# Diagonal queries and keys of stick-breaking attention in separate tiles, queries loaded through SyncE; the scan written in place

## The chip, the cores and the metric

The kernel runs on one core of a Trainium2 chip. The core's engines are TensorE (PE; its weight loads are listed as PEld), VectorE (DVE), ScalarE (ACT), GpSimd (POOL) and SyncE (SP), which here only issues transfers. The metric is the device time of one execution in microseconds, and lower is better. The kernel before takes 2462.47 us (median of three runs, 2457.55 to 2462.65).

## The reference

One layer of a hybrid encoder in float32, on 2048 positions of width 1024. A shared RMSNorm and one input projection feed three mixers: a short gated convolution (A), a gated convolution of width 31 with LayerNorm and swish (B), and stick-breaking attention with 8 heads of width 64 (C). Their outputs are concatenated, projected and added to the input; then come a second RMSNorm, an MLP with squared ReLU (width 4096), the residual and a last RMSNorm. The change lies in C, which is strictly causal:

```python
z = jnp.einsum("bhqd,bhkd->bhqk", qb, kb) * scale
mask = s_idx < t_idx
log_beta = jax.nn.log_sigmoid(z)
log_1m = jnp.where(mask, log_beta - z, 0.0)
suffix = lax.cumsum(log_1m, axis=3, reverse=True) - log_1m
a = jnp.where(mask, jnp.exp(log_beta + suffix), 0.0)
outs.append(jnp.einsum("bhqk,bhkd->bhqd", a, vb))
```

So a weight is sigmoid(z) times the product of sigmoid(-z) over all later keys that the query may see.

## The kernel before

**Numbers.** Matrix products are made with float32 operands split in a high and a low part (`split`: ScalarE writes the high part, VectorE or GpSimd the rest), three products each (`mm3`, L99). In attention the scores take two matmuls per key tile (L513 with the queries' high part, L514 with the low part); the high and low parts of the keys share the 128 partitions, 64 rows each.

**Stages.** `p_start` and `p_half(0)` project the first 1024 positions, `p_half(1)` the second; K, Q and V go to DRAM (KQ, VS). Beside `p_half(1)` runs attention for the first block of 512 queries (i = 0, one group per head). Then `block(tb)` does the output projection and the MLP of the four blocks of 512 positions, and beside blocks 0 to 2 runs attention for the query blocks 1 to 3. Main work and attention are interleaved by `weave`, which advances each side generator by costs written out by hand. The order of instructions on each engine, and when a tile's buffer changes hands, is then worked out ahead of time by a planner (`schedule_with_timeline_sim=True`, L1102), and each engine runs its own list in order. A transfer that waits for a buffer holds up what stands behind it in the same engine's list.

**A group** is one head h and one query block i. `attention` (L700) alternates the steps of the current group's first pass with those of the previous group's second pass.

- `a_load` (L487): one tile KQd of 128 x 3 x 512 holds the keys of the diagonal block and both parts of the queries. It has one buffer. It is loaded by two transfers of 384 KB (one for each half of the partitions) in GpSimd's queue (`load_r`, L81). The call stands at the end of the loop over the steps of the group before.
- `a_pass1` (L537): loads Kl, the keys before the diagonal (one buffer, GpSimd's queue, L549). Three steps follow for the diagonal: scores, two sigmoids and masks (`a_diag`, L522: t holds sigmoid(z), om holds sigmoid(-z)), and products of om. The products over all keys of a position's group go into a tile Rd, its left half at L557 in the first step, its right half at L573 in the third. Then `a_cross_a` runs, and for i > 0 there are 4 i further steps, each with one key tile of Kl (L584 to L598), and a second `a_cross_a` at L599. The queries of KQd are read up to the last of these steps, its keys in the first three only.
- `a_cross_a` (L601): clears one column of a tile T on GpSimd (L605), transposes Rd or R into it (L606, VectorE, 32 x 32 blocks), runs a multiplicative scan from T into a tile O (L609), multiplies the pieces of the four partition groups in C (L617), and writes O times C back into T (L623). T has a buffer T1 for the diagonal and T2 for the rest.
- `a_pass2` (L627): loads V, transposes T into PSUM (L641), multiplies it onto the stored t, splits the result (Ahi, Alo) and multiplies it with V (`a_av`, L682).

The buffers of om are two, shared with the tile otmp of pass 2 (L667).

Of the kernel before, what the change touches and what calls it, by code (L numbers as in the profile page):

```python
# [68 lines left out]
class Trunk:  # L69
# [414 lines left out]
        own = slice(HD * (h % 2), HD * (h % 2) + HD)  # L484
        return [(slice(HD * part, HD * part + HD), self.KQ[h // 2, part, own]) for part in range(2)]

    def a_load(self, h, i):  # L487
        q0 = TB * i
        pool = self.at
        g = {"h": h, "i": i}  # L490
        t = pool.tile([P, 3, TB], F32R, name="KQd", tag="KQd", bufs=self.ab["KQd"])
        for rows, kq in self.kq_halves(h):
            to = t[rows].rearrange("c a (j q) -> c (a j) q", j=2)
            self.load_r(to, kq.rearrange("c a j q -> c (a j) q")[:, :, q0 // 2 : (q0 + TB) // 2])
        g["Kd"], g["qh"], g["ql"] = t[:, 0], t[:, 1], t[:, 2]
        return g

    def v_load(self, g):
        pool, i = self.at, g["i"]
# [37 lines left out]
    def a_pass1(self, g):  # L537
        nc, pool, i = self.nc, self.at, g["i"]
        ab = self.ab
        lo, hi2 = slice(0, 256), slice(256, 512)  # L540

        def new(name, bufs, shape=(P, TB), dt=F32):
            return pool.tile(list(shape), dt, name=name, tag=name, bufs=bufs)

        if i:
            g["Kl"] = pool.tile([P, self.kmax], F32R, name="Kl", tag="Kl", bufs=self.ab["Kl"])
            for rows, kq in self.kq_halves(g["h"]):
                to = g["Kl"][rows, : TB * i].rearrange("c (j q) -> c j q", j=2)
                self.load_r(to, kq[:, 0, :, : TB * i // 2])  # L549
        A0 = g["A0"] = []  # L550
        Rd = new("Rd", 1)

        k2 = [g["Kd"][:, 0:P], g["Kd"][:, 256 : 256 + P]]
        z = self.a_z(g, [(k2[1], lo, lo), (k2[0], lo, hi2)])
        t, om = self.a_diag(z, 0)
        nc.gpsimd.tensor_tensor(t[:, hi2], t[:, hi2], om[:, lo], op=ALU.mult)
        nc.vector.tensor_tensor(Rd[:, lo], om[:, lo], om[:, hi2], op=ALU.mult)  # L557
        A0.append(t)
        yield 1

        k4 = self.every(g["Kd"], 4)
        z = self.a_z(g, [(k4[3], hi2, lo), (k4[2], hi2, hi2)])
        t, om = self.a_diag(z, 1)
        nc.gpsimd.tensor_tensor(t[:, hi2], t[:, hi2], om[:, lo], op=ALU.mult)
        R = new("R", 2)
        nc.vector.tensor_tensor(R[:, lo], om[:, lo], om[:, hi2], op=ALU.mult)
        A0.append(t)
        yield 1
        z = self.a_z(g, [(k4[1], hi2, lo), (k4[0], hi2, hi2)])
        t, om = self.a_diag(z, 2)  # L570
        nc.vector.tensor_tensor(R[:, hi2], om[:, lo], R[:, lo], op=ALU.mult)
        nc.gpsimd.tensor_tensor(t, t, R, op=ALU.mult)
        nc.vector.tensor_tensor(Rd[:, hi2], om[:, hi2], R[:, hi2], op=ALU.mult)  # L573
        A0.append(t)
        yield 1
        tot = self.a_cross_a(g, Rd, None)
        if not i:
            return
        J = 4 * i
        kl = self.every(g["Kl"][:, : TB * i], J)  # L580
        full = slice(0, TB)
        R = None
        for j in range(J - 1, -1, -1):
            z = self.a_z(g, [(kl[j], full, full)])  # L584
            t = new("A0", ab["A0"])
            if R is None:
                nc.scalar.activation(t, z, AF.Sigmoid, scale=0.125)
                R = new("R", 2)
                nc.scalar.activation(R, z, AF.Sigmoid, scale=-0.125)
            else:  # L590
                nc.scalar.activation(t, z, AF.Sigmoid, scale=0.125)  # L591
                nc.scalar.activation(z, z, AF.Sigmoid, scale=-0.125)  # L592
                nc.gpsimd.tensor_tensor(t, t, R, op=ALU.mult)  # L593
                Rn = new("R", 2)
                nc.vector.tensor_tensor(Rn, z, R, op=ALU.mult)  # L595
                R = Rn
            A0.append(t)
            yield 1  # L598
        self.a_cross_a(g, R, tot)  # L599

    def a_cross_a(self, g, R, seed):  # L601

        nc, pool = self.nc, self.at
        T = pool.tile([P, 16, 33], F32, name="T", tag="T1" if seed is None else "T2", bufs=1)
        nc.gpsimd.memset(T[:, :, 32:33], 0.0)  # L605
        nc.vector.transpose(T[:, :, 0:32], R)  # L606
        O = pool.tile([P, 16, 33], F32, name="O", tag="O", bufs=1)
        fl = lambda x: x.rearrange("p a b -> p (a b)")[:, ::-1]
        nc.vector.tensor_tensor_scan(fl(O), fl(T), fl(self.d1), 1.0, op0=ALU.mult, op1=ALU.add)  # L609
        C = self.tiny.tile([P, 16], F32, name="C", tag="C", bufs=3)  # L610
        if seed is None:
            nc.gpsimd.memset(C[96:128], 1.0)
        else:
            nc.vector.tensor_copy(C[96:128], seed)
        for a in (2, 1, 0):
            s, d = slice(32 * a + 32, 32 * a + 64), slice(32 * a, 32 * a + 32)
            nc.vector.tensor_tensor(C[d], C[s], O[s, :, 0], op=ALU.mult)  # L617
        tot = None
        if seed is None:
            tot = self.tiny.tile([32, 16], F32, name="tot", tag="tot", bufs=2)  # L620
            nc.vector.tensor_tensor(tot, C[0:32], O[0:32, :, 0], op=ALU.mult)
        qt = T[:, :, 0:32]
        nc.vector.tensor_tensor(qt, O[:, :, 1:33], C.unsqueeze(2).to_broadcast([P, 16, 32]), op=ALU.mult)  # L623
        g["qd" if seed is None else "ql"] = qt
        return tot

# [72 lines left out]

    def attention(self, groups):  # L700
        prev = None
        nxt = self.a_load(*groups[0])
        for n in range(len(groups) + 1):
            g, nxt = nxt, None
            p1 = self.a_pass1(g) if g else iter(())
            p2 = self.a_pass2(prev) if prev else iter(())
            n1 = 3 + 4 * g["i"] if g else 0
            n2 = 3 + 4 * prev["i"] if prev else 0
            d1 = d2 = 0.0
            live1, live2 = g is not None, prev is not None  # L710
            loaded = False
            while live1 or live2:
                if live2 and (not live1 or d2 * max(n1, 1) <= d1 * max(n2, 1)):
                    try:
                        next(p2)
                        d2 += 1
                        yield 0.5
                    except StopIteration:
                        live2 = False
                elif live1:  # L720
                    try:
                        next(p1)
                        d1 += 1
                        yield 0.5
                    except StopIteration:
                        live1 = False
                if not loaded and self.ab["KQd"] > 1 and d1 >= n1 / 2 and n + 1 < len(groups):
                    nxt = self.a_load(*groups[n + 1])
                    loaded = True
            if not loaded and n + 1 < len(groups):  # L730
                nxt = self.a_load(*groups[n + 1])
            prev = g


# [276 lines left out]
    def build(self):  # L1011
        tc = self.tc
        with ExitStack() as ctx:
# [6 lines left out]
            with ExitStack() as c1:  # L1020
                self.psum_pool(c1, d=3, c=1, z=2, q=1, o=1)
                self.p_pools(c1)
                self.w_eng = "dve"
                self.sb = 2
                self.xl = [[None] * DC for _ in range(2)]
                self.xh = [[None] * DC for _ in range(2)]
                with tc.tile_pool(name="raw0", bufs=1) as self.rp:
                    self.rb, self.rt = 21, "raw"
                    self.p_start()
                self.rp = self.raw  # L1030
                self.rb, self.rt = self.xb, "xt"
                self.at = c1.enter_context(tc.tile_pool(name="at1", bufs=1))
                self.ab = dict(KQd=1, Kl=1, A0=5, om=2, Alo=2, Ahi=2, Vl=1, late=1, yc=2)
                weave(self.p_half(0), [(Side(self.mixer_b(0)), 83, 20, 225, True), (Side(self.x_norms()), 24, 60, 180, True)])
                self.heads = {}
                a0 = Side(self.attention([(h, 0) for h in range(H)]))
                weave(self.p_half(1), [(Side(self.mixer_b(1)), 98, 0, 200, True), (a0, 28, 0, 210, True), (Side(self.pre_split()), len(self.presplit), 0, 200, True)])
            with ExitStack() as c2:
# [4 lines left out]
                self.hp = c2.enter_context(tc.tile_pool(name="hp", bufs=1, reuse_waits="tile"))  # L1043
                self.ob = 2
                self.kmax = 1536
                self.ab = dict(KQd=1, Kl=1, A0=15, om=2, Alo=3, Ahi=3, Vl=2, late=2, yc=1)
                at = Side(self.attention([(h, i) for i in (1, 2, 3) for h in range(H)]))
                self.heads = {}

# [56 lines left out]
```

## Time and profile before

| | us |
|---|---|
| median of three runs | 2462.47 |
| the profiled execution's own time | 2461.45 |
| its span, first to last instruction | 2459.7 |
| TensorE busy | 2397.3 |
| VectorE busy | 1629.8 |
| GpSimd busy | 1139.2 |
| ScalarE busy | 1032.8 |

The mean granted clock of TensorE is 0.991. The transfers move 549.04 MB, 223 GB/s on average; SyncE's queue takes 56.0% of the 16 DMA engines' time and GpSimd's 15.8%. Attention's first scores run at 227 us and its last at 1964 us.

Rows of the profile are read as follows. A group of instructions is "line engine operation, out<-in, shapes, xcount", then busy us and mean ns of one, then the idle time of the engine just before and what ended it. A row "PE ps_z L513 <- DMA KQd<-KQ" tells what an engine waited for: us in total, times, longest. A row of a timeline has start and length in us, and in brackets the idle time before it and its releaser. A row of a window has the stretch, its length, then busy us and count for PE, PEld, DVE, ACT and POOL, and last the granted clock of TensorE (1.00 is full speed), the DMA share and GB/s. A name such as KQd<-KQ is a transfer, its times counted from issue to landing.

### The profile page before, as it was taken

What the parts mean: (1) busy time and instruction counts of PE and PEld (TensorE: products, weight loads), DVE (VectorE), ACT (ScalarE), POOL (GpSimd) and SP (SyncE); (2) the same over time, 40 slices, a digit from 0 to 9 for tenths busy, and PEclk for the clock granted to TensorE, in tenths of its full rate; (3) what the DMA queues carried; (4) which work ended last, traced back from release to release, by engine and by line L of the source; (5) the groups of instructions that cost most, each with busy time, mean ns of one, the idle gap of its engine ahead of it and who ended that gap; (6) DMA issues with size and microseconds to landing.
All of it is one profiled execution on the core that took longest, in us unless ns stands there. A gap on an engine that the chain in (4) does not pass through costs nothing.

```text
span 2459.7 us, 32438 instructions
## 1 busy us (share of the span) xinstructions
PE 2397.3 (97%) x11316; PEld 2016.1 (82%) x11316; DVE 1629.8 (66%) x2372; ACT 1032.8 (42%) x1910; POOL 1139.2 (46%) x1197
## 2 busy tenths in 40 slices
PE   8999989999999999999999999999999999999998
PEld 7888877898778878787878888888888888788887
DVE  7958599953898878867877768576666735212114
ACT  5232432232656656534555555345555532121121
POOL 0343256640667666515766677168887830000000
PEclk9999999999999999999999999999999999999999
DMA  7579897687688977787877777776666656655555
GB/s 260 190 257 311 285 301 202 210 276 234 180 223 236 243 217 196 184 275 242 250 221 246 228 227 204 264 222 186 187 204 189 199 180 201 240 196 184 202 188 189
DMA packets 236035, 549.04 MB, mean 223 GB/s; under 512 B 25696, under 2 KB 99424, under 8 KB 217440
## 3 DMA queue, kind: packets, MB, share of 16 engines
q1 hardware_dynamic: 179792, 472.50, 56.0%
q0 software_dynamic: 53888, 73.42, 15.8%
q8 instruction: 90, 1.47, 0.2%
q10 hardware_dynamic: 2192, 1.05, 0.2%
q14 instruction: 73, 0.60, 0.1%
HBM read 390.38 MB, written 148.11 MB: 219 GB/s over the span
## 4 chain that ended last, share of the span: by engine, by line
PE 72%; DVE 13%; DMA 9%; issue 3%; POOL 2%; ACT 1%; SPq 0%; POOLq 0%; DVEq 0%; ACTq 0%
PE ps_y L103 8%; PE ps_u L103 8%; PE ps_u L105 8%; PE ps_y L107 8%; PE ps_u L107 8%; PE ps_y L105 8%; PE ps_p L103 3%; PE ps_p L105 3%; PE ps_p L107 3%; DMA KQd<-KQ 2%; PE ps_z L513 2%; DVE ps_c L450 2%; PE ps_z L514 2%; PE ps_x L103 2%; PE ps_x L105 2%
## 5 line engine op out<-in xcount | busy, mean ns | idle before, releaser
L90 POOL TENSOR_TENSOR Alo<-A,Ahi 128x512 fp32r<-128x512 f32 x288 | 399.1, 1397 | 102.0 <-PE ps_o L698 43.8
L940 DVE TENSOR_TENSOR acc<-acc,ps_y 128x512 f32<-128x512 f32 (+1 forms) x264 | 174.7, 666 | 179.6 <-PE ps_y L107 178.3
L103 PE MATMUL ps_y<-fh,w 128*128 128x512 f32 (+1 forms) x1056 | 283.5, 386 | 8.4 <-DVE acc L940 4.7
L103 PE MATMUL ps_u<-hh,w 128*128 128x512 f32 x1024 | 279.5, 393 | 7.4 <-DMA w<-s_w 5.0
L107 PE MATMUL ps_y<-fl,w 128*128 128x512 f32 (+1 forms) x1056 | 278.6, 383 | 1.5 <-DVE fl L915 1.5
L105 PE MATMUL ps_y<-fh,w 128*128 128x512 f32 (+1 forms) x1056 | 279.5, 384 | 0.0
L593 POOL TENSOR_TENSOR A<-A,R 128x512 f32<-128x512 f32 x168 | 233.1, 1389 | 94.6 <-ACT A L591 70.7
L105 PE MATMUL ps_u<-hh,w 128*128 128x512 f32 x1024 | 276.9, 392 | 0.0
L107 PE MATMUL ps_u<-hl,w 128*128 128x512 f32 x1024 | 276.4, 390 | 0.0
L118 POOL TENSOR_TENSOR rs_y<-rs_v,mhalf 128x4 f32<-128x4 f32 (+1 forms) x13 | 14.5, 1115 | 546.1 <-DVE rs_v L117 486.0
L905 ACT ACTIVATE ps_u<-ps_u 128x512 f32<-128x512 f32 x128 | 74.7, 584 | 455.8 <-PE ps_u L107 455.8
L103 PEld LDWEIGHTS ps_y<-fh,w 128*128 128x128 f32 x1056 | 193.8, 189 | 47.9 <-DVE fl L915 4.5
L103 PEld LDWEIGHTS ps_u<-hh,w 128*128 128x128 f32 x1024 | 190.7, 189 | 47.5 <-DMA w<-s_w 7.2
L107 PEld LDWEIGHTS ps_y<-fl,w 128*128 128x128 f32 x1056 | 195.0, 188 | 41.4 <-DVE fl L915 2.5
L105 PEld LDWEIGHTS ps_y<-fh,w 128*128 128x128 f32 x1056 | 195.5, 189 | 39.8
L105 PEld LDWEIGHTS ps_u<-hh,w 128*128 128x128 f32 x1024 | 193.3, 189 | 41.4 <-DVE w L90 0.2
L107 PEld LDWEIGHTS ps_u<-hl,w 128*128 128x128 f32 x1024 | 192.4, 188 | 40.1
L915 DVE TENSOR_TENSOR fl<-ps_u,fh 128x512 fp32r<-128x512 f32 x128 | 87.5, 684 | 193.3 <-ACT fh L914 192.8
L595 DVE TENSOR_TENSOR R<-ps_z,R 128x512 f32<-128x512 f32 x168 | 115.4, 687 | 147.2 <-ACT ps_z L592 106.6
L88 ACT ACTIVATE Ahi<-A 128x512 fp32r<-128x512 f32 x288 | 177.2, 628 | 82.2 <-PE ps_o L697 35.9
L450 DVE SCALAR_TENSOR_TENSOR ps_c<-g,wb,ps_c 128x512 f32<-128x512 f32 x240 | 179.9, 750 | 4.7
L88 ACT ACTIVATE w<-wraw 128x512 fp32r<-128x512 f32 x152 | 91.9, 628 | 175.2 <-PE ps_y L107 113.1
(173 smaller groups left out, 4928.4 us busy)
## 6 DMA issues: line engine op xcount, KB each, us to landing
w<-s_w SPq DMA_DIRECT2D x200, 512.0 KB, 3.4
w<-s_w SPq DMA_DIRECT2D x68, 1024.0 KB, 4.8
wraw<-in_w SPq DMA_DIRECT2D x192, 256.0 KB, 4.7
w<-s_w_out SPq DMA_DIRECT2D x64, 512.0 KB, 5.0
s_w<-w SPq DMA_DIRECT2D x32, 1024.0 KB, 5.7
s_w<-w SPq DMA_DIRECT2D x56, 512.0 KB, 4.6
KQd<-KQ POOLq DMA_DIRECT2D x64, 384.0 KB, 6.9
xraw<-in_xT SPq DMA_DIRECT2D x48, 256.0 KB, 5.0
```

What stands on the lines that cost most here:

```text
L88: nc.scalar.activation(hi, x, AF.Copy)
L90: e.tensor_tensor(lo, x, f(hi), op=ALU.subtract)
L103: self.nc.tensor.matmul(ps, wh, xh, start=start and k == 0, stop=False)
L105: self.nc.tensor.matmul(ps, wl, xh, start=False, stop=False)
L107: self.nc.tensor.matmul(ps, wh, xl, start=False, stop=stop and k == n - 1)
L450: nc.vector.scalar_tensor_tensor(t, g[:, k : k + TB], self.wb[:, c, k : k + 1], t, op0=ALU.mult, op1=ALU.add)
L513: nc.tensor.matmul(z[:, oc], keys, g["qh"][:, qc], start=k == 0, stop=False)
L593: nc.gpsimd.tensor_tensor(t, t, R, op=ALU.mult)
L595: nc.vector.tensor_tensor(Rn, z, R, op=ALU.mult)
L905: nc.scalar.activation(ps, ps, AF.Relu)
L915: nc.vector.tensor_tensor(lo, ps, f(hi), op=ALU.subtract)
L940: nc.vector.tensor_tensor(acc[d][:, cols], acc[d][:, cols], ps, op=ALU.add)
```

## The change

Three things are changed.

1. KQd becomes two tiles. Qd (both parts of the queries, 128 x 2 x 512) has two buffers and is loaded by `a_queries` in SyncE's queue; Kd (the diagonal's keys, 128 x 512) has one and is loaded by `a_keys` in GpSimd's queue. The queries of the next group are asked for after the first step of the current group's pass 1, its keys after the third.
2. Rd is gone. The two products are written over om's right half, and each half is transposed into T as soon as it is there, so that T is taken in the first step and the diagonal's one transpose of 128 x 512 becomes two of 128 x 256.
3. O is gone. The scan and the product with C are written over T.

In SBUF a partition holds 4 KB more for the queries and the keys (10 instead of 6), 2 KB less for Rd and 2.1 KB less for O.

```diff
-    def a_load(self, h, i):
-        q0 = TB * i
-        pool = self.at
-        g = {"h": h, "i": i}
-        t = pool.tile([P, 3, TB], F32R, name="KQd", tag="KQd", bufs=self.ab["KQd"])
+    def a_queries(self, h, i):
+        q0 = slice(TB * i // 2, TB * i // 2 + TB // 2)
+        q = self.at.tile([P, 2, TB], F32R, name="Qd", tag="Qd", bufs=2)
         for rows, kq in self.kq_halves(h):
-            to = t[rows].rearrange("c a (j q) -> c (a j) q", j=2)
-            self.load_r(to, kq.rearrange("c a j q -> c (a j) q")[:, :, q0 // 2 : (q0 + TB) // 2])
-        g["Kd"], g["qh"], g["ql"] = t[:, 0], t[:, 1], t[:, 2]
-        return g
+            self.dma(q[rows].rearrange("c a (j q) -> c (a j) q", j=2), kq[:, 1:3].rearrange("c a j q -> c (a j) q")[:, :, q0])
+        return {"h": h, "i": i, "qh": q[:, 0], "ql": q[:, 1]}
+
+    def a_keys(self, g):
+        q0 = slice(TB * g["i"] // 2, TB * g["i"] // 2 + TB // 2)
+        g["Kd"] = self.at.tile([P, TB], F32R, name="Kd", tag="Kd", bufs=1)
+        for rows, kq in self.kq_halves(g["h"]):
+            self.load_r(g["Kd"][rows].rearrange("c (j q) -> c j q", j=2), kq[:, 0, :, q0])
...
-        Rd = new("Rd", 1)
...
-        nc.vector.tensor_tensor(Rd[:, lo], om[:, lo], om[:, hi2], op=ALU.mult)
+        nc.vector.tensor_tensor(om[:, hi2], om[:, lo], om[:, hi2], op=ALU.mult)
+        T = pool.tile([P, 16, 33], F32, name="T", tag="T1", bufs=1)
+        nc.gpsimd.memset(T[:, :, 32:33], 0.0)
+        nc.vector.transpose(T[:, 0:8, 0:32], om[:, hi2])
...
-        nc.vector.tensor_tensor(Rd[:, hi2], om[:, hi2], R[:, hi2], op=ALU.mult)
+        nc.vector.tensor_tensor(om[:, hi2], om[:, hi2], R[:, hi2], op=ALU.mult)
+        nc.vector.transpose(T[:, 8:16, 0:32], om[:, hi2])
...
-        tot = self.a_cross_a(g, Rd, None)
+        tot = self.a_cross_a(g, T, None)
...
-        self.a_cross_a(g, R, tot)
+        T = pool.tile([P, 16, 33], F32, name="T", tag="T2", bufs=1)
+        nc.gpsimd.memset(T[:, :, 32:33], 0.0)
+        nc.vector.transpose(T[:, :, 0:32], R)
+        self.a_cross_a(g, T, tot)
...
-        nc.vector.tensor_tensor_scan(fl(O), fl(T), fl(self.d1), 1.0, op0=ALU.mult, op1=ALU.add)
+        nc.vector.tensor_tensor_scan(fl(T), fl(T), fl(self.d1), 1.0, op0=ALU.mult, op1=ALU.add)
...
-            nc.vector.tensor_tensor(C[d], C[s], O[s, :, 0], op=ALU.mult)
+            nc.vector.tensor_tensor(C[d], C[s], T[s, :, 0], op=ALU.mult)
...
-        qt = T[:, :, 0:32]
-        nc.vector.tensor_tensor(qt, O[:, :, 1:33], C.unsqueeze(2).to_broadcast([P, 16, 32]), op=ALU.mult)
+        qt = T[:, :, 1:33]
+        nc.vector.tensor_tensor(qt, qt, C.unsqueeze(2).to_broadcast([P, 16, 32]), op=ALU.mult)
...
     def attention(self, groups):
         prev = None
-        nxt = self.a_load(*groups[0])
+        nxt = self.a_queries(*groups[0])
+        self.a_keys(nxt)
...
-                if not loaded and self.ab["KQd"] > 1 and d1 >= n1 / 2 and n + 1 < len(groups):
-                    nxt = self.a_load(*groups[n + 1])
-                    loaded = True
-            if not loaded and n + 1 < len(groups):
-                nxt = self.a_load(*groups[n + 1])
+                if nxt is None and d1 >= 1 and n + 1 < len(groups):
+                    nxt = self.a_queries(*groups[n + 1])
+                if nxt and "Kd" not in nxt and d1 >= 3:
+                    self.a_keys(nxt)
```

More of the change, by code (lines that the diff above doesn't have):

```diff
@@ L598, in a_pass1, with a_cross_a @@
             yield 1
-        self.a_cross_a(g, R, tot)
-    def a_cross_a(self, g, R, seed):
-        nc, pool = self.nc, self.at
-        T = pool.tile([P, 16, 33], F32, name="T", tag="T1" if seed is None else "T2", bufs=1)
+        T = pool.tile([P, 16, 33], F32, name="T", tag="T2", bufs=1)
         nc.gpsimd.memset(T[:, :, 32:33], 0.0)
         nc.vector.transpose(T[:, :, 0:32], R)
-        O = pool.tile([P, 16, 33], F32, name="O", tag="O", bufs=1)
+        self.a_cross_a(g, T, tot)
+    def a_cross_a(self, g, T, seed):
+        nc = self.nc
         fl = lambda x: x.rearrange("p a b -> p (a b)")[:, ::-1]
-        nc.vector.tensor_tensor_scan(fl(O), fl(T), fl(self.d1), 1.0, op0=ALU.mult, op1=ALU.add)
+        nc.vector.tensor_tensor_scan(fl(T), fl(T), fl(self.d1), 1.0, op0=ALU.mult, op1=ALU.add)
         C = self.tiny.tile([P, 16], F32, name="C", tag="C", bufs=3)
@@ L620, in a_cross_a @@
             tot = self.tiny.tile([32, 16], F32, name="tot", tag="tot", bufs=2)
-            nc.vector.tensor_tensor(tot, C[0:32], O[0:32, :, 0], op=ALU.mult)
-        qt = T[:, :, 0:32]
-        nc.vector.tensor_tensor(qt, O[:, :, 1:33], C.unsqueeze(2).to_broadcast([P, 16, 32]), op=ALU.mult)
+            nc.vector.tensor_tensor(tot, C[0:32], T[0:32, :, 0], op=ALU.mult)
+        qt = T[:, :, 1:33]
+        nc.vector.tensor_tensor(qt, qt, C.unsqueeze(2).to_broadcast([P, 16, 32]), op=ALU.mult)
         g["qd" if seed is None else "ql"] = qt
@@ L710, in attention @@
             live1, live2 = g is not None, prev is not None
-            loaded = False
             while live1 or live2:
@@ L1032, in build @@
                 self.at = c1.enter_context(tc.tile_pool(name="at1", bufs=1))
-                self.ab = dict(KQd=1, Kl=1, A0=5, om=2, Alo=2, Ahi=2, Vl=1, late=1, yc=2)
+                self.ab = dict(Kl=1, A0=5, om=2, Alo=2, Ahi=2, Vl=1, late=1, yc=2)
                 weave(self.p_half(0), [(Side(self.mixer_b(0)), 83, 20, 225, True), (Side(self.x_norms()), 24, 60, 180, True)])
@@ L1045, in build @@
                 self.kmax = 1536
-                self.ab = dict(KQd=1, Kl=1, A0=15, om=2, Alo=3, Ahi=3, Vl=2, late=2, yc=1)
+                self.ab = dict(Kl=1, A0=15, om=2, Alo=3, Ahi=3, Vl=2, late=2, yc=1)
                 at = Side(self.attention([(h, i) for i in (1, 2, 3) for h in range(H)]))
```

## The prediction

> **What bounds the kernel now.** I read the busy shares of the page first, then the waits of TensorE, because an engine that is busy for 97% of the span can only be helped by what it still waits for.
>
> ```profile
> span 2459.7 us, 32438 instructions
> PE 2397.3 (97%) x11316; PEld 2016.1 (82%) x11316; DVE 1629.8 (66%) x2372; ACT 1032.8 (42%) x1910; POOL 1139.2 (46%) x1197
> ```
>
> TensorE is idle for 2459.7 - 2397.3 = 62.4 us in all. The change removes no matmul, so nearly all that it can gain lies in those 62.4 us. The view of who waited for whom, for TensorE alone (total us, times, longest), names them:
>
> ```profile
> PE ps_z L513 <- DMA KQd<-KQ: 12.5, 8, 3.6
> PE ps_o L689 <- ACT Ahi L88: 8.1, 3, 6.0
> PE ps_v L397 <- DVE vt L405: 6.3, 3, 3.9
> PE ps_u L103 <- DMA w<-s_w: 5.0, 5, 1.7
> PE ps_y L103 <- DVE acc L940: 4.7, 4, 2.5
> ```
>
> The reader is to see that the longest entry is the one load which the change splits: eight times the first score matmul of a head group stood waiting for KQd. The other entries are for conversions, weights and accumulators, which the change does not touch directly.
>
> Why the load is late is seen in one group. The first two lines are TensorE's timeline (last scores of the old group, first of the next), then GpSimd's at the same place (start, length, idle before):
>
> ```profile
> 1218.47 0.39 PE L514 MATMUL ps_z<-KQd,Kl 128*128 128x512 f32 x1
> 1234.33 0.36 PE L513 MATMUL ps_z<-KQd 128*128 128x256 f32 x1 [3.63 <-DMA KQd<-KQ]
> ...
> 1219.17 1.36 POOL L83 DMA_DIRECT2D KQd<-KQ  x2 [2.00 <-PE ps_z L514]
> 1220.52 1.20 POOL L83 DMA_DIRECT2D Kl<-KQ  x2
> ```
>
> KQd has one buffer, and the queries in it are read by the last score matmul. So the load can't start before 1218.9, GpSimd issues it at 1219.17, and TensorE was ready for the next group's first scores at 1234.33 - 3.63 = 1230.7, 11.5 us after that. The data were there at 1234.3, 15.2 us after the issue.
>
> The wait has a second part that the list doesn't show. These are stretches of 4 us (busy time of PE, PEld, DVE, ACT, POOL, then the granted clock, DMA share, GB/s) from 496, 900, 904, 1232 and 1236 us:
>
> ```profile
> 496.00:500.00 4.00, 1.94 (x10) 1.06 (x9) 3.86 (x9) 1.56 (x3) 2.56 (x3) 1.00 1.06 351
> 900.00:904.00 4.00, 3.95 (x13) 3.25 (x14) 3.94 (x7) 1.63 (x4) 0.13 (x1) 0.61 1.10 298
> 904.00:908.00 4.00, 4.00 (x22) 3.40 (x22) 3.90 (x6) 2.40 (x6) 2.26 (x3) 0.96 1.05 409
> 1232.00:1236.00 4.00, 1.68 (x12) 1.71 (x13) 2.92 (x5) 0.92 (x2) 0.25 (x1) 0.92 1.28 263
> 1236.00:1240.00 4.00, 4.00 (x14) 3.20 (x14) 2.13 (x4) 3.12 (x7) 3.92 (x7) 0.65 0.59 173
> ```
>
> Behind the waits that end at 900.05 and at 1234.33 the granted clock falls: (0.39 + 0.04) x 4 = 1.72 us lost, and (0.08 + 0.35) x 4 = 1.72 us. That time counts as busy. Of the eight waits only these two are followed by it; behind the 2.06 us wait that ends at 499.4 the clock stayed at 1.00.
>
> The Trainium skill (TensorE: Matmul & The Clock Gate, Part 1) says that the clock halves after an idle window of about 3.4 us. By that rule only the 3.63 us wait would carry the loss, and the gain below would be 1.7 us smaller; the trace differs, since the row of 900 us stands behind a wait of 2.37 us, and I go by the trace.
>
> **The change part by part.**
>
> *The split load.* The KQd wait goes if each part is there in time. Queries (128 KB a half, two halves) are in two buffers, so their load needs only the score matmuls of the group before the current one, a whole group earlier. Keys of the diagonal are read only by the first three score tiles, so their single buffer is free after the third step, and the load is issued then. The group of 1234.33 us is followed by one at 1285.74, 51 us later (first row below), so both loads have tens of us where 15 sufficed.
>
> ```profile
> 1285.74 0.28 PE L513 MATMUL ps_z<-KQd 128*128 128x256 f32 x1
> KQd<-KQ POOLq DMA_DIRECT2D x64, 384.0 KB, 6.9
> DMA to landing us min/median/max: 4.5/6.9/17.1
> ```
>
> Even the longest landing, 17.1 us, fits. In the eight groups of block 0 a group has only three steps; there the keys get one step more than before and the queries a whole group. Gain: 12.5 + 2 x 1.72 = 15.9 us. What is late next: for the same 12 score matmuls, nothing but a free PSUM bank; for the tiles behind them, Kl (in the rivals).
>
> *DMA issues.* The issues go from 64 to 128, the bytes stay. GpSimd keeps 64 (keys alone) and SyncE gets 64 for the queries.
>
> ```profile
> L83 POOL DMA_DIRECT2D KQd<-KQ x64: 653/688/947, 189.7 to 1907.9; - x64
> 1189.84 0.32 SPq L79 DMA_DIRECT2D w<-s_w  x1
> SPq L79 <- PE ps_u L107: 387.1, 148, 5.2
> POOL KQd L83 <- PE ps_z L514: 37.1, 8, 24.6
> ```
>
> SyncE: 64 x 0.32 = 20 us more issue time, beside waits of 387.1 us for one releaser alone, so the time is there; I take 0 for it, and come back to the order of its queue. GpSimd: the 37.1 us for which it stood in front of the KQd load go, but it is busy for 46% of the span and none of the longer waits of TensorE is for it: 0.
>
> *No Rd.* The two products are written over om, same shape, same engine: 0. The transpose of 128x512 becomes two of 128x256.
>
> ```profile
> L606 DVE STREAM_TRANSPOSE T<-Rd x32: 696/711/714, 237.3 to 1929.6; 128x512 f32<-128x512 f32 x32
> L573 DVE TENSOR_TENSOR Rd<-om,R x32: 424/426/1514, 235.8 to 1929.2; 128x256 f32<-128x256 f32 x32
> L595 DVE TENSOR_TENSOR R<-ps_z,R 128x512 f32<-128x512 f32 x168 | 115.4, 687 | 147.2 <-ACT ps_z L592 106.6
> ```
>
> No row shows a transpose of 256. Ends: half of 711 each (0 more), or 711 each (32 x 0.711 = 22.8 us of VectorE). A 256 product takes 426 ns against 687 for 512, a ratio of 0.62, so I take 0.44 us each: 32 x (0.88 - 0.71) = 5.4 us. Where VectorE is nearly full this reaches the end. The first row below is the stretch from 300 to 400 us, VectorE at 93.61; the second is TensorE's wait for KQd between 220 and 450 us alone:
>
> ```profile
> 300.00:400.00 100.00, 91.13 (x413) 73.86 (x411) 93.61 (x144) 29.67 (x59) 50.41 (x57) 0.97 0.89 279
> PE ps_z L513 <- DMA KQd<-KQ: 0.7, 2, 0.5
> ```
>
> There run groups of block 0, of which there are eight: 8 x 0.17 = 1.4 us, which I charge in full (upper end 8 x 0.71 = 5.7). In the other 24 groups VectorE has idle time and the rest costs nothing. Half of the transposing also moves ahead of the third step, so the scan starts some 0.27 us earlier; no wait hangs on that, 0. The T memset (GpSimd) moves up in the text by two steps; its tile was last read at the first step of pass 2 of the group before, which comes earlier still: 0.
>
> *om held longer.* Its buffer is free one transpose later. ScalarE waits for it now:
>
> ```profile
> ACT om L527 <- DVE Rd L557: 40.7, 12, 5.3
> ```
>
> Twelve waits of 0.44 us more are 5.3 us of ScalarE, behind which Ahi and the FFN's squares queue, for which TensorE and VectorE wait. ScalarE is busy for 42%, so I take 0 and keep 5.3 us as the upper end.
>
> *Scan and product in place.* Same shapes (the scan takes 1490 ns, the product 674):
>
> ```profile
> L609 DVE TENSOR_TENSOR_SCAN O<-T,d x56: 1232/1490/7669, 238.0 to 1967.8; 128x528 f32<-128x528 f32 x56
> L623 DVE TENSOR_TENSOR T<-O,C x56: 670/674/2227, 243.2 to 1973.3; 128x512 f32<-128x512 f32 x56
> L940 DVE TENSOR_TENSOR acc<-acc,ps_y 128x512 f32<-128x512 f32 (+1 forms) x264 | 174.7, 666 | 179.6 <-PE ps_y L107 178.3
> ```
>
> No row has a scan in place; acc, a product-sized operation in place, takes 666 ns against 674 for one that isn't. I take 0, with 1% either way (56 x 2.16 us x 1% = 1.2 us). The order on VectorE already serialises all users of O and T, so no wait is added.
>
> **Sum**, against the profiled execution's 2461.45 us (span 2459.7 plus 1.75 around it): 2461.45 - 12.5 - 3.4 + 1.4 + 0.7 = 2447.6. The 0.7 is the part of the KQd wait in 220 to 450 us, where VectorE is full: a wait lifted there comes back as one for VectorE. This execution lies 1.0 us under the median of 2462.47, so I forecast **2449 us**, 0.55% under it.
>
> **The rivals.**
>
> *Half is given back (2457).* Kl takes KQd's place. It still has one buffer and still waits for the last score matmul, and it lands late:
>
> ```profile
> Kl<-KQ POOLq DMA_DIRECT2D x16, 256.0 KB, 10.2
> PE ps_z L513 <- DMA Kl<-KQ: 0.3, 1, 0.3
> 1243.86 0.40 PE L513 MATMUL ps_z<-KQd,Kl 128*128 128x512 f32 x1
> ```
>
> In the group above Kl is issued at 1220.5 and first used at 1243.9, 23.4 us later. If the diagonal now runs up to 11 us earlier, 12 us remain against 10.2 of landing, and some groups wait. Against it: with queries and most of the keys out of the way only Kl is moved at that moment, and GpSimd reaches it 1.36 us earlier. If the waits are half the old ones and om's 5.3 us reaches TensorE in part (2 us), 2448.6 + 6.2 + 2 = 2457. The whole of both gives 2448.6 + 12.5 + 5.3 = 2466.
>
> *Slower (2473).* The queries stand in SyncE's queue, in order with the weights. Their load waits for the last scores of the group before; if SyncE gets there before TensorE does, the weights behind it wait too, and TensorE for them. GpSimd's row shows how long such a wait can be, at the change from one block to the next:
>
> ```profile
> 1100.95 1.35 POOL L83 DMA_DIRECT2D KQd<-KQ  x2 [24.56 <-PE ps_z L514]
> 1218.70 1.09 PE L103 MATMUL ps_u<-hh,w 128*128 128x512 f32 x4
> 1224.19 0.39 PE L697 MATMUL ps_o<-Ahi,Vl 128*128 128x512 f32 x1
> w<-s_w SPq DMA_DIRECT2D x200, 512.0 KB, 3.4
> ```
>
> 24 matmuls of the FFN take 1224.19 - 1218.70 = 5.5 us and use two of the four weight buffers; so weights are some 11 us ahead, 7.6 after their landing of 3.4. Shorter blocks than 7.6 us cost nothing, as seven of the eight waits did at (37.1 - 24.6) / 7 = 1.8 us on average. One of 24.6 us that falls where no weights are ahead, at the block's beginning, costs it all: 2448.6 + 24.6 = 2473. Decisive is whether more than 13.9 + 4.9 = 18.8 us of such blocks come through. Against it: with two buffers the scores waited for are a group back, some 40 to 60 us.
>
> The Trainium skill (DMA: Bandwidth & Descriptors, Issuing engines are not separate DMA queues) says that transfers from all issuing engines run on the same 16 DMA engines; by it the move to SyncE brings no bandwidth and only the order can cost, which is this rival's price, not another one.
>
> *It does not do what it says (2462).* The keys' load on GpSimd could be issued late all the same, behind Alo and A, and the first scores would wait for Kd as for KQd: 2461.45 + 1.4 = 2463, within 0.2% of before. Against it: behind the third step of a group of 51 us the keys still have some 30 us.
>
> **Chances.** Forecast 0.64, half given back 0.18, SyncE's queue 0.13, no effect 0.05. What a measurement of this kernel can tell from no change is 0.2%, about 4.9 us: faster is below 2457.5. The second case straddles that bound; of its 0.18 I count 0.05 as faster, 0.10 as within 0.2% and 0.03, near its full price, as slower: faster 0.64 + 0.05 = 0.69, same 0.10 + 0.05 = 0.15, slower 0.03 + 0.13 = 0.16. The range reaches down to 2440 (no VectorE cost, and half of the 13.1 us of waits for Ahi and weights going with the freed GpSimd and ScalarE) and up to 2466, the full price of the second case.
>
> **What would show it.** Right: no wait of TensorE for the queries or for Kd, TensorE idle near 50 us, no clock loss behind a group's first scores. Transposes of 256 at 0.36 to 0.5 us. Wrong: a row of ps_z waiting for Kl above 5 us (second case); ps_u waiting for weights well above 5.0 us, with SyncE waiting for ps_z ahead of the Qd loads (third); waits for Kd (fourth). The largest doubt is the order of all engines, which is planned ahead: another plan may bring waits in other places, such as the one of 6.0 us for Ahi, which no row of before can tell.

## The result, and the profile after

| | before | after |
|---|---|---|
| median, us (22 runs each) | 2461.16 | 2466.85 |
| lowest and highest, us | 2454.69 to 2469.54 | 2457.0 to 2476.12 |
| profiled execution, us | 2461.45 | 2470.28 |
| ratio of times, 95% interval | | 1.003, 1.0019 to 1.0042 |

The change made the kernel slower by 0.3%. The forecast was 2449, faster by 0.55%, with a range from 2440 to 2466. Both programs' single executions scatter over some 15 to 19 us, so times are compared by medians and by the interval of the ratio.

The head of the page after, TensorE's waits (total us, times, longest), and two groups of VectorE:

```profile
span 2468.6 us, 32575 instructions
PE 2398.0 (97%) x11316; PEld 2015.1 (82%) x11316; DVE 1641.6 (67%) x2404; ACT 1031.1 (42%) x1910; POOL 1125.6 (46%) x1197
...
PE ps_o L695 <- ACT Ahi L88: 11.4, 6, 4.2
PE ps_y L103 <- DVE acc L946: 6.9, 5, 3.4
PE ps_p L311 <- ACT wh L88: 6.4, 1, 6.4
PE ps_z L516 <- DVE R L601: 6.2, 5, 2.4
PE ps_v L397 <- DVE vt L405: 4.6, 3, 3.4
PE ps_y L103 <- DVE fl L921: 4.1, 2, 2.9
PE ps_u L103 <- DMA w<-s_w: 4.0, 4, 2.3
PE ps_o L695 <- DVE yc L678: 3.9, 3, 1.4
PE ps_y L107 <- DVE fl L921: 3.6, 3, 2.7
PE ps_z L516 <- ACT A L531: 3.5, 1, 3.5
PE ps_x L103 <- DMA w<-s_w_out: 3.3, 3, 2.0
PE ps_z L516 <- DMA Kd<-KQ: 2.2, 1, 2.2
...
L562 DVE STREAM_TRANSPOSE T<-om x32: 416/434/447, 230.8 to 1933.1; 128x256 f32<-128x256 f32 x32
L615 DVE TENSOR_TENSOR_SCAN T<-T,d x56: 1231/1758/4690, 240.7 to 1978.0; 128x528 f32<-128x528 f32 x56
```

The reader is to see three things. The wait for the load fell from 12.5 us in eight places to 2.2 us in one. TensorE is idle for 2468.6 - 2398.0 = 70.6 us all the same, where it was 62.4. And the entries that grew most are for results of VectorE and ScalarE: the scores wait for R (6.2, before 0.4) and for the sigmoid of the diagonal (3.5, before none), attention's products for Ahi (11.4, before 8.1) and for yc (3.9, before none).

Between 1114 and 1132 us, at the beginning of a block, one such wait can be followed through the engines. These are VectorE's, ScalarE's and TensorE's timelines after (start, length, idle before), and stretches of 4 us with the clock ahead of the last two columns:

```profile
1114.44 10.13 DVE L967 TENSOR_TENSOR acc<-acc,ms 128x512 f32<-128x512 f32 x5
...
1125.10 1.15 DVE L967 TENSOR_TENSOR acc<-acc,ms 128x512 f32<-128x512 f32 x1
1126.17 0.41 DVE L559 TENSOR_TENSOR om<-om 128x256 f32<-128x256 f32 x1
1126.51 0.41 DVE L571 TENSOR_TENSOR R<-om 128x256 f32<-128x256 f32 x1
...
1127.01 0.60 ACT L530 ACTIVATE om<-ps_z 128x512 f32<-128x512 f32 x1 [7.38 <-DVE R L571]
1127.51 0.59 ACT L531 ACTIVATE A<-ps_z 128x512 f32<-128x512 f32 x1
...
1128.15 0.81 PE L516 MATMUL ps_z<-Qd,Kl 128*128 128x512 f32 x1 [3.50 <-ACT A L531]
...
1120.00:1124.00 4.00, 3.96 (x11) 3.15 (x12) 4.00 (x3) 0.00 (x0) 3.97 (x6) 0.61 0.75 239
1124.00:1128.00 4.00, 0.65 (x3) 0.15 (x1) 3.27 (x6) 0.99 (x3) 2.02 (x2) 0.93 0.73 192
1128.00:1132.00 4.00, 3.85 (x11) 3.14 (x12) 0.00 (x0) 4.00 (x9) 2.15 (x3) 0.61 0.02 8
```

The block's products acc x ms occupy VectorE until 1126; the group's products of om stand behind them in its list. ScalarE waits 7.38 us for om's buffer, so the third diagonal tile's sigmoid runs at 1127.5, so its PSUM bank (the piece of memory that TensorE writes its sums to) is free only then, and TensorE stands 3.50 us in front of the next scores. Around that the granted clock drops: the three stretches lose (0.39 + 0.07 + 0.39) x 4 = 3.4 us, as much as the prediction had counted as regained behind the load's waits.

The same place before, VectorE's, ScalarE's and TensorE's timelines:

```profile
1115.48 13.30 DVE L961 TENSOR_TENSOR acc<-acc,ms 128x512 f32<-128x512 f32 x8
...
1129.80 0.60 ACT L527 ACTIVATE om<-ps_z 128x512 f32<-128x512 f32 x1 [2.62 <-DVE Rd L557]
...
1118.85 0.39 PE L513 MATMUL ps_z<-KQd 128*128 128x256 f32 x1 [1.11 <-DMA KQd<-KQ]
1132.67 0.40 PE L513 MATMUL ps_z<-KQd,Kl 128*128 128x512 f32 x1
```

VectorE was as late, and the third sigmoid ran even later, at 1129.8. But the group began at 1118.85, after a wait of 1.11 us for KQd, and the scores that need the bank stood at 1132.67 in TensorE's list, with the MLP's matmuls ahead of them: no wait. In the changed kernel they stand at 1128.15, 4.5 us earlier in time.

### The profile page after: what moved, and what is told of

It is laid out like the page before. It is cut to its first block, busy times and chain, and to the rows that moved or that the text cites. A ratio compares the mean times of both kernels' runs of the same rounds, so it can differ in the third digit from the quotient of the medians.

```text
span 2468.6 us, 32575 instructions
## 1 busy us (share of the span) xinstructions
PE 2398.0 (97%) x11316; PEld 2015.1 (82%) x11316; DVE 1641.6 (67%) x2404; ACT 1031.1 (42%) x1910; POOL 1125.6 (46%) x1197
## 4 chain that ended last, share of the span: by engine, by line
PE 64%; DVE 20%; DMA 9%; issue 4%; ACT 2%; POOL 1%; SPq 0%; DVEq 0%; POOLq 0%; ACTq 0%
PE ps_y L103 8%; PE ps_y L107 8%; PE ps_y L105 8%; PE ps_u L103 7%; PE ps_u L105 7%; PE ps_u L107 7%; DVE ps_c L450 3%; DVE A L657 2%; PE ps_p L103 2%; PE ps_p L105 2%; PE ps_p L107 2%; DVE T L615 2%; DVE C L623 2%; PE ps_z L516 2%; PE ps_x L103 2%
## 5 line engine op out<-in xcount | busy, mean ns | idle before, releaser
L103 PE MATMUL ps_y<-fh,w 128*128 128x512 f32 (+1 forms) x1056 | 284.4, 387 | 11.2 <-DVE acc L946 6.9
L599 POOL TENSOR_TENSOR A<-A,R 128x512 f32<-128x512 f32 x168 | 226.8, 1352 | 97.1 <-ACT A L597 61.4
L90 DVE TENSOR_TENSOR w<-wraw,w 128x512 fp32r<-128x512 f32 x152 | 153.5, 1031 | 28.5 <-ACT w L88 28.1
```

The source lines that it names most:

```text
L90: e.tensor_tensor(lo, x, f(hi), op=ALU.subtract)
L103: self.nc.tensor.matmul(ps, wh, xh, start=start and k == 0, stop=False)
```

## The experiments

Four theories were put up, one after the other. **A**: operands that are there early let TensorE run into the score banks and VectorE's products; the split load is the cause. **B**: om and T are held longer and VectorE has more to do; the edits in place are the cause. **C**: any change makes the planner order all engines anew, and each order has waits of its own. **D**, formed after the runs of other orders and before those with VectorE relieved: what is gained at the load is taken back by waits for VectorE because VectorE is late.

The order itself can be changed without touching an instruction, a tile or a queue: the number 45 in the last line of `build` says where in a block attention begins. Other numbers ("orders" below) give other lists.

```diff
-weave(self.block(tb, self.end), [(at, (74, 95, 107)[tb], 45, 365 if tb < 2 else 320, False)] if tb < 3 else [])
+weave(self.block(tb, self.end), [(at, (74, 95, 107)[tb], 47, 365 if tb < 2 else 320, False)] if tb < 3 else [])
```

**The edits in place alone** (inplace_only). The load stays as before: `a_load`, KQd, and the end of the loop in `attention`. The lines show one place of it, against the changed kernel.

```diff
-        nxt = self.a_queries(*groups[0])
-        self.a_keys(nxt)
+        nxt = self.a_load(*groups[0])
```

> The edits without Rd and O alone; queries and keys stay one tile KQd with one buffer, loaded by GpSimd. Theory A (operands that are there early let TensorE run into the score banks and VectorE's products; the split is the cause): TensorE waits 10 to 14 us for KQd again, its waits of ps_z for VectorE's R and ScalarE stay under 2.5 us, and the time is that of before within 4 us. Theory B (om and T are held longer, VectorE has 5 us more to do; the edits in place are the cause): the wait for KQd stays near 12 us, the waits of TensorE for Ahi, fl, acc and R grow by 8 us or more over before, time 2468 to 2475. Theory C (any new order of the engines moves the waits about): TensorE's waits fall on other lines than in either kernel, time anywhere within 8 us of before.

Measured: 2471.42 us, ratio to the kernel before 1.0049 (1.0032 to 1.0066). Its waits of TensorE, the three that decide:

```profile
PE ps_z L513 <- DMA KQd<-KQ: 12.6, 9, 2.9
PE ps_z L513 <- DVE R L598: 2.2, 3, 0.8
PE ps_y L103 <- DVE fl L918: 5.1, 2, 4.7
```

The load's wait is back, as all theories say, and the bank's is small, as A says; but the time is B's. The waits that B named (Ahi, fl, acc and R) rose from 20.6 to 25.2 us, by 4.6 where B asked for 8 or more; with Alo and yc they rose from 21.8 to 29.1.

**Another order of both kernels** (before_nudge, after_nudge: 47).

> The kernel before with one number of the interleaving changed, 45 to 47 (where in a block attention begins), which leaves every instruction, tile and queue as it was and only makes another order. Theory C: the sum of TensorE's waits moves by 4 us or more, and the time by 3 to 8 us either way. Theories A and B: time within 3 us of before, the wait for KQd still the largest, 9 to 16 us.

> The changed kernel with the same number changed, 45 to 47. Theory A: the waits of ps_z for VectorE's R and for ScalarE stay at 6 to 14 us, time 2464 to 2470, above before by 0.1 to 0.4%. Theory B: waits for Ahi, fl and acc stay at 22 to 30 us together, same time. Theory C: the waits change their lines, and the time may as well come out under before (2455 to 2475).

Measured: before 2466.66 us, ratio 1.0029 (1.0016 to 1.0043); after 2452.82 us, ratio 0.9976 (0.9964 to 0.9989), both against before at 45. So C: two units in one number made one kernel slower by some 6 us and the other faster by some 14. At this order the change gains 13.8 us. TensorE's waits in the two, before at 47 first, after at 47 second:

```profile
PE ps_z L513 <- DMA KQd<-KQ: 15.8, 8, 4.0
PE ps_z L513 <- DVE R L595: 3.6, 3, 2.0
```

```profile
PE ps_y L103 <- DVE fl L921: 8.1, 4, 2.8
PE ps_y L103 <- DVE acc L946: 6.0, 9, 1.5
PE ps_z L516 <- DMA Kd<-KQ: 1.1, 1, 1.1
```

Neither R nor the sigmoid of the diagonal holds up the scores in after_nudge: A's wait is not a rule. The waits for acc and fl are larger in it nevertheless; Ahi, fl and acc together are at 25.9, inside B's range, but the time is not B's.

**One buffer for the queries** (after_q1).

```diff
-        q = self.at.tile([P, 2, TB], F32R, name="Qd", tag="Qd", bufs=2)
+        q = self.at.tile([P, 2, TB], F32R, name="Qd", tag="Qd", bufs=1)
```

> The changed kernel with one buffer for the queries in place of two, so that their load must wait for the last scores of the group as KQd's did; keys, queues and the edits in place stay. Theory A: TensorE waits 8 to 14 us for Qd, the waits of ps_z for R and for ScalarE fall from 9.7 us to under 3, time at or under before (2455 to 2463). Theory B: waits for Qd come back on top of the others, time 2474 or more. Theory C: no rule, within 8 us of before.

Measured: 2476.17 us, ratio 1.0068 (1.0048 to 1.0088).

```profile
PE ps_z L516 <- DMA Qd<-KQ: 26.2, 14, 4.0
PE ps_z L516 <- DMA w<-wraw: 5.0, 1, 5.0
```

A fails again in its time and in the size of the wait for Qd (26.2 against 8 to 14), and C's range (within 8 us of before) is missed too; B's time came, but not as B says, on top of the other waits. R and the sigmoid are gone from the scores' waits, but the time rose by 9 us. The two buffers are what removes the wait; SyncE's queue alone doesn't.

This run shows most directly that waits are exchanged. Nothing but when the queries may be loaded was changed, and the order that the planner makes of it: the load's wait rose from 2.2 to 26.2 us, and the waits for results fell from 41.0 to 19.7, under the 22.1 of the kernel before. All waits together rose by only 2.4 us; the rest of the longer time is TensorE's busy time (2404.3 us against 2398.0), at a granted clock of 0.988 against 0.993. Two rows that had grown with the change are back at 3.3 and 2.3 us, from 6.9 and 4.1:

```profile
PE ps_y L103 <- DVE acc L946: 3.3, 5, 1.1
PE ps_y L103 <- DVE fl L921: 2.3, 1, 2.3
```

**More orders** (43, 41 and 50 of before and after; 43 and 47 of the edits in place). The edit is the same number.

> The kernel before with attention begun at 43 in place of 45, nothing else. Theory C (each order has waits of its own, some 3 to 8 us either way, whatever the edit): time 2455 to 2470, KQd still waited for 10 to 16 us, the rest of the waits moved by 4 us or more. Theory B (the loss comes from the edits in place, and the order matters little): 2458 to 2463.

> The edits without Rd and O alone, attention begun at 43. Theory B: 8 to 12 us above before_43, as at 45, where it was 11 us. Theory C: anywhere from 5 us under to 12 us above before_43; KQd waited for 10 to 16 us either way.

> The whole change, attention begun at 43. The forecast's step (the wait for the load and the clock behind it go, 12 to 16 us) together with Theory C: TensorE waits under 3 us for Kd and Qd, time 8 to 20 us under inplace_43 and 0 to 14 us under before_43. Theory A (the bank wait takes its place): ps_z waits 6 to 14 us for VectorE or ScalarE, time within 3 us of inplace_43 and above before_43.

> The edits in place alone, attention begun at 47, where before took 2466.7 us and the whole change 2452.8. Theory B: 2475 to 2479 (8 to 12 us above before). Theory C: 2460 to 2475. Either way 12 us or more above the whole change, since KQd is waited for again.

> The kernel before with attention begun at 50. So far before took 2460 at 45, 2467 at 47 and 2477 at 43. If 45 was a lucky order for it (Theory C): 2462 to 2478, KQd waited for 11 to 20 us. If the loss of the change is a rule (A or B) and the orders near 45 were unlucky: 2456 to 2462.

> The whole change with attention begun at 50. Every order so far leaves it under 3 us of wait for Qd and Kd. Theory C with the wait given back in part (other waits of TensorE 4 to 20 us above those of before at the same number): 0 to 14 us under before_50. Theory A: above before_50, with 6 us or more of ps_z waiting for VectorE or ScalarE.

> The kernel before with attention begun at 41. As at 50: 2462 to 2478 if 45 was a lucky order, 2456 to 2462 if not; KQd waited for 11 to 20 us.

> The whole change with attention begun at 41. As at 50: under 3 us for Qd and Kd; Theory C 0 to 14 us under before_41, Theory A above it.

Measured, each ratio against the kernel before at 45 on the same chip; medians of different chips are not to be compared. The last three columns are sums over the rows of TensorE's waits in one profiled execution, in us: for KQd, Qd, Kd and Kl (the load); of ps_z, ps_o, ps_y and ps_u for VectorE's, ScalarE's or GpSimd's results (a few V and issue waits among them, up to 2.9 us); and all rows.

| kernel | order | median us (runs) | ratio, interval | load | results | all |
|---|---|---|---|---|---|---|
| before | 41 | 2457.74 (10) | 0.9997, 0.9979 to 1.0015 | 11.8 | 15.3 | 50.6 |
| before | 43 | 2476.51 (4) | 1.0072, 1.0046 to 1.0098 | 17.8 | 25.6 | 66.4 |
| before | 45 | 2461.16 (22) | 1 | 12.8 | 22.1 | 56.0 |
| before | 47 | 2466.66 (12) | 1.0029, 1.0016 to 1.0043 | 15.8 | 22.4 | 60.5 |
| before | 50 | 2472.73 (9) | 1.0056, 1.0037 to 1.0076 | 20.1 | 23.0 | 67.8 |
| after | 41 | 2450.59 (10) | 0.9963, 0.9943 to 0.9983 | 0 | 32.5 | 50.5 |
| after | 43 | 2473.00 (4) | 1.0067, 1.0042 to 1.0091 | 0.7 | 43.4 | 64.1 |
| after | 45 | 2466.85 (22) | 1.0030, 1.0019 to 1.0042 | 2.2 | 41.0 | 64.0 |
| after | 47 | 2452.82 (12) | 0.9976, 0.9964 to 0.9989 | 1.1 | 28.5 | 50.2 |
| after | 50 | 2474.36 (6) | 1.0065, 1.0042 to 1.0088 | 0 | 37.5 | 60.3 |
| after, one query buffer | 45 | 2476.17 (6) | 1.0068, 1.0048 to 1.0088 | 26.2 | 19.7 | 66.4 |
| in place | 43 | 2467.67 (9) | 1.0034, 1.0020 to 1.0049 | 12.8 | 29.6 | 62.4 |
| in place | 45 | 2471.42 (10) | 1.0049, 1.0032 to 1.0066 | 12.6 | 31.7 | 64.8 |
| in place | 47 | 2467.67 (5) | 1.0049, 1.0029 to 1.0070 | 20.2 | 23.8 | 63.5 |

Three readings. The order alone moves the kernel before over 0.75% (0.9997 to 1.0072) and the changed one over 1.04% (0.9963 to 1.0067), more than the change. The ratio of after less that of before at the same order is -0.34, -0.05, +0.30, -0.53 and +0.09% for 41 to 50: mean -0.11%, standard error 0.15 (from the scatter of the five). The wait for the load fell in all five, on average from 15.7 to 0.8 us; the waits for results rose in all five, from 21.7 to 36.6 (from 20.6 to 36.5 without the V and issue waits). Theory B falls: the ratio of the edits in place less that of before is +0.49% at 45, +0.20 at 47 and -0.38 at 43. Of the rise in waits for results at 43 to 47 (23.4 to 28.4 to 37.6 on average), one third came with the edits in place and two thirds with the split load.

No theory forecast every one of these runs. At 43 the kernel before lay above C's range (2476.51 against 2455 to 2470), the edits in place lay 8.8 us under it where C allowed 5, and the whole change lay 5.3 us above them where 8 to 20 below was expected; there the scores waited 9.2 us for R and the sigmoid, as A says, but the time was under before, which A excludes. At 41 the kernel before took 2457.74, where C had expected 2462 or more. At 50 the whole change was 1.6 us above before, where C had it below.

**VectorE relieved** (four kernels). Without the product of the stored weights with Q for key tiles off the diagonal, the output lacks that factor.

```diff
-            else:
-                nc.vector.tensor_tensor(t, t, Q, op=ALU.mult)
```

> The kernel before without VectorE's product of the stored weights with Q for the tiles off the diagonal (192 of 0.68 us, 117 us of VectorE); its output lacks that factor. It relieves VectorE and nothing else beside blocks 0 to 2. Theory D (what the change gains at the load is taken back by waits for VectorE's results): TensorE waits less for acc, fl and Ahi than in before, KQd still 11 to 20 us, time 2445 to 2460. Theory C (only the order): any wait may move, time 2445 to 2470.

> The whole change without the same product. Theory D: with VectorE relieved the gain at the load stays: 10 to 16 us under before_noq_45 (at 45 the whole change was 6 us above before), waits of ps_y and ps_u for acc and fl at most 4 us above those of before_noq_45. Theory C: the difference is as much by chance as the others, from 14 us under to 6 us above.

> As before_noq_45 with attention begun at 50: 2445 to 2465, KQd waited for 11 to 20 us.

> The whole change without the same product, begun at 50. Theory D: 10 to 16 us under before_noq_50 (with the product it was 2 us above before_50). Theory C: from 14 us under to 6 us above.

Measured: at 45, before 2458.16 us (ratio 0.9995, 0.9984 to 1.0007) and after 2446.94 (0.9955, 0.9941 to 0.9968): 11.2 us faster, as D says. At 50, before 2452.58 (0.9974, 0.9961 to 0.9988) and after 2458.28 (1.0000, 0.9984 to 1.0016): 5.7 us slower, against D. VectorE was busy for 1535 to 1555 us in the four. TensorE's waits for acc and fl in after at 45 without the product, and the load's wait in before at 45 without it:

```profile
PE ps_y L103 <- DVE fl L919: 5.0, 3, 3.3
PE ps_y L103 <- DVE acc L944: 2.6, 2, 2.0
```

```profile
PE ps_z L513 <- DMA KQd<-KQ: 18.2, 10, 3.5
```

All waits but the load's rise from before to after by 8.4 us at 45 and 7.3 at 50, where the same two orders with the product have 18.6 and 12.6. So a relieved VectorE takes back less, but not so clearly that the time follows at both orders. At 50 the two profiled executions (2458.21 and 2447.67 us) differ the other way than the medians: the second is the lowest of its ten, so its waits don't speak for the median. D stays open.

**The same two kernels a second time** (before_again, after_again, no edit, one execution each).

> The kernel before, unchanged, profiled a second time: how far do TensorE's waits of one and the same order differ between two executions? If the differences between the orders are theirs (Theory C), this one repeats the first profile: KQd 10 to 16 us, the other waits within 4 us of 43.2 in sum. If one execution alone moves the waits by 8 us or more, single profiles of two orders can't be compared by their sums.

> The whole change, unchanged, profiled a second time: under 3 us for Qd and Kd, the other waits within 4 us of 61.8 in sum if they belong to the order, 8 us or more away if they belong to the execution.

Measured: 2455.38 and 2469.68 us. All waits but the load's: 43.3 us (43.2 the first time) and 64.1 us (61.8). The rows come back too, among them the one of the block's beginning:

```profile
PE ps_z L516 <- ACT A L531: 5.9, 1, 5.9
PE ps_z L516 <- DVE R L601: 5.8, 5, 2.4
```

So in both pairs the waits belong to the order and not to the single execution, and sums of two orders may be compared. What differs between two executions of one order is elsewhere: the kernel before took 6.1 us less the second time, and TensorE's busy time was 5.4 us less (2391.9 against 2397.3).

**The fastest** is the whole change at 41: 2450.59 us, 0.9963 (0.9943 to 0.9983) of the kernel before, and 0.67% under the changed kernel at 45. Before at 41 gives no such gain (0.9997).

## Why the prediction was wrong

The sign was wrong and the time lay outside the range. By its own steps:

- *The wait for the load goes, and the clock loss behind it.* Right in its mechanism and nearly in size: 12.5 us became 2.2 here, and no stretch of 4 us between 656 and 1120 us, nor between 1132 and 1640, has a lowered clock any more. The load's part held in every order. The clock's part, 2 x 1.72 us, is not shown: in the second execution of the kernel before, the wait of 3.15 us that ends at 1232.9 is followed by no loss and the one of 1.83 us that ends at 493.5 by (0.25 + 0.18) x 4 = 1.72 us, so which waits it follows is not fixed by the order; and the changed kernel loses 3.4 us at 1120 to 1132. TensorE's busy time, which holds these losses, went from 2397.3 to 2398.0, and its idle time to 70.6 where some 50 were forecast.
- *Transposes of 256 at 0.44 us.* Right: 434 ns (445 for the right half).
- *Scan and product in place at nothing.* Right in sum: the 56 scans took 102.4 us where they had taken 105.8, though their median is higher in place (1758 ns against 1490, and so in every order). What lengthened the median was not traced. VectorE's busy time rose by 11.8 us in this pair where 5.4 were counted, and by 6.2 on average over the five orders. The scans before, then after (the first number behind the bar is their sum):

```profile
L609 DVE TENSOR_TENSOR_SCAN O<-T,d 128x528 f32<-128x528 f32 x56 | 105.8, 1890 | 1.1
L615 DVE TENSOR_TENSOR_SCAN T<-T,d 128x528 f32<-128x528 f32 x56 | 102.4, 1828 | 1.2
```

- *SyncE's issue at 0.32 us.* Mis-sized: 0.59 us for a half of Qd, and the half is 256 KB, not 128 (the keys' halves are 128). It cost nothing that was seen; the slower rival, SyncE's queue, did not come: waits for weights were 7.5 us against 5.7.
- *"What is late next: for the same 12 score matmuls, nothing but a free PSUM bank".* This is the step that failed: it named the bank, priced it and every result behind it at nothing, and gave no reason. The sum took 15.9 us for the wait and gave back 0.7 + 1.4. The bank was late (R and A, 9.7 us against 0.4), and so were the other results. In the profiled pair, the load's waits fell by 10.6 us, and those of ps_z, ps_o, ps_y and ps_u for results rose from 22.1 to 41.0; over five orders 14.9 us were gained and 14.9 given back there, with 2.4 us gained in all rows. TensorE in order, without its stops at the load, comes to the next result earlier than VectorE or ScalarE delivers it. One buffer for the queries brings the stops back, and the waits for results fall to 19.7. That VectorE's lateness is the reason for the whole of the rise was not shown: relieving it halved the rise at the two orders tried and kept the gain at one of them.
- *The rival that gives half back* had the right shape and the wrong engine: not Kl (no wait for it in the five orders, 0.8 us at most with VectorE relieved) but the results.
- *"another plan may bring waits in other places".* Named as the largest doubt and not priced. It is what decides the sign at 45: the order that the kernel before has at 45 is 0.3 to 0.7% faster than its orders at 43, 47 and 50, and only 41 equals it; the changed kernel's order at 45 is 0.5 to 0.7% slower than its orders at 41 and 47, and some 0.4% faster than at 43 and 50. With 47 in both kernels the same change gains 0.53%, and the forecast of 0.55% would have looked right, by luck of the order. A range widened by some 0.5% for that alone would have held the time.

Settled: the load's wait is removed, nearly as much waiting comes up elsewhere, and the change as such is worth -0.11% with an error of 0.15%, which can't be told from nothing, and is not the forecast's -0.55%. Open: how much of the given-back time is VectorE's lateness, and how much the orders'. The split load without the edits in place was not tried; with two buffers for the queries it takes 4 KB more of each partition, and no run shows whether there is room.

## What to carry to other kernels

Where one engine is busy for 97% and runs a list fixed in advance, a wait taken away need not be time gained: the engine arrives earlier at the next result, so look for what is late there before the wait is counted. Where a planner orders the engines, an edit is compared over several orders of both kernels; one order of each compares two draws. A tuned constant belongs to the kernel it was tuned on, and is tried again after an edit.

## What the runs showed of the hardware

Issuing a half of Qd (256 KB in 64 rows, four runs of 1 KB each) took 0.59 us in SyncE's queue, and a weight piece of 512 or 1024 KB took 0.32 us (medians):

```profile
L79 SPq DMA_DIRECT2D Qd<-KQ x64: 573/586/1266, 190.9 to 1852.3; - x64
L79 SPq DMA_DIRECT2D w<-s_w x268: 319/319/2375, 604.1 to 2449.1; - x134
```

VectorE's product acc x ms, 128x512 with both operands in SBUF, has a median of 688 ns, but the five that begin at 1114.44 us took 10.13 us together. One of them took 5.79 us, one 1.77, two 1.10 and one 0.68, and GpSimd was busy almost without a gap all the while (3.97 of 4 us in the stretch from 1120):

```profile
1116.49 5.79 DVE L967 TENSOR_TENSOR acc<-acc,ms 128x512 f32<-128x512 f32 x1
```

It is these products that held up the group in the timeline above. Since short ones ran beside the busy GpSimd too, its being busy does not by itself explain the long one; why it is slow was not tried.
